# A hybrid decoder layer on one core: the last attention phases' filler work is regrouped around scores and value products

## The chip, the core and the metric

The kernel runs on one core of a Trainium2 chip. A core has a matrix engine (TensorE, PE in the profile, with PEld for its weight loads), a vector engine (DVE), a scalar engine (ACT), GpSimd (POOL) and SyncE (SP), which issues this kernel's transfers. The metric is the device time of one launch in microseconds. It was 1298.78 us as the median of three runs (1298.3 to 1299.28).

## The reference

One decoder layer on 1024 tokens of width 1024, all in float32. A joint projection gives the inputs of two groups of causal attention heads: eight sparse heads (NSA) and four differential heads. Their joined outputs go through an output projection, a residual with layer norm, a SwiGLU feed-forward part of width 2816, and a second layer norm. The change touches the differential heads and what runs beside them:

```python
def diff_attention(q, k, v, lq1, lk1, lq2, lk2, subln_g, slopes, lam_init):
    lam = exp(sum(lq1 * lk1)) - exp(sum(lq2 * lk2)) + lam_init
    ...
    def block(args):                      # one block of 128 query rows
        s = einsum('bqhcd,bkhcd->bhcqk', q_blk, k) * scale
        s = s - slopes[None, :, None, None, None] * dist
        p = masked_softmax(s, dist >= 0)
        a = p[:, :, 0] - lam * p[:, :, 1]
        return einsum('bhqk,bkhe->bqhe', a, v)
    ...
    o = rms_norm(o, subln_g) * (1.0 - lam_init)
...
mix = concatenate([o_diff, o_nsa], axis=-1) @ w_out[l]
x = layer_norm(DEEPNORM_ALPHA * x + mix, ln1_g[l], ln1_b[l])
ffn = (silu(x @ w_gate[l]) * (x @ w_up[l])) @ w_down[l]
x = layer_norm(DEEPNORM_ALPHA * x + ffn, ln2_g[l], ln2_b[l])
```

A head thus has two softmaxes per query block, and their difference is multiplied with the values.

## The kernel before

**Precision.** A product that needs full float32 is split: each operand into a high and a low part, three matmuls per product (`mm3`, lines 116 to 118). `split` writes the parts: a cast on ACT (line 81), a subtraction on DVE or POOL (line 83). `load_split_here` issues the load on SP (line 99) and then splits.

**Units.** The differential attention of head h works in units: one per block i of 128 query rows (row i below), i from 0 to 7, on `(i + 1) * 128` keys. A unit has a front and a back.

- The front makes the scores of both softmaxes into `psS` banks (two matmuls each, lines 331 and 334; past 512 keys in two halves). DVE evacuates each bank with the mask and the row minimum (line 340), ACT takes the exponential (line 354), DVE makes the weight `r1` of the second softmax (lines 475 and 476). The two are then summed: the first five eighths of the width on DVE (line 478), the rest on POOL in two steps (480, 481).
- The back transposes the sum (line 363 into `psT`, ACT copies it, 366), multiplies it with the values into `psO` (line 493), and evacuates the result: DVE copies it (497), ACT sums its squares (498). Behind four rows of a head, `finish` does the RMS norm: small steps on DVE (506 to 508), a power on POOL (509), a multiplication on DVE (510), transposes on TensorE (513), and the store of the transposed rows to `mix_d`.

There are two `psS` banks, two `psM`, three `psT` and one `psO`.

**Fillers.** Other matmuls run beside the units: the projections of q, k and values of later heads, and the output projection of the first rows. Each is a generator that yields after a few matmuls with its cost. `q_fill` (called `qdf` for these heads) projects a q half, ACT scales it (line 176), DVE makes the low part (line 177), and three moves by SP bring the parts to the partitions where the scores read them (line 161). `dvf` projects value rows (matmuls of 256 columns into `psM`). `wo_fill` loads and splits the output weights, `out_fill` makes one block of output rows in two halves of 512 columns, each over `psM`. `held_fill` and `ln_fill` hold back the RMS norms and run layer norms.

**The order.** A table `phases` lists units with their fillers. For each unit the planner calls the front, and runs the back of the unit that is `look` units older; during the back it pumps fillers in proportion to the planned cost of the unit (`ahead`, and `later`, a delay of priority). Units still pending at the end of a phase are carried over to the next. With `passed[0]` a number n, a projection's matmuls are placed behind the score issued n before the last one (`proj_mm3`); with `None` they are free. In the phases marked `even = False`, carried-over units have a weight of zero, so no filler is shared over them. A scheduler then fixes each engine's program from priorities and its own estimate of times; what it makes of the table shows only in the instruction order.

**The last phases** are: head 2 rows 0 to 3; head 3 rows 0 to 3 with the second half of head 2's q and four value rows as fillers; head 2 rows 4, 7, 6, 5 with both halves of w_out, the second half of head 3's q and two blocks of output rows; head 3 rows 4 to 7 with layer norms and two more output blocks. The output projection of the other blocks and the feed-forward part follow.

## Time and profile before

| | before |
|---|---|
| median of three runs | 1298.78 us (1298.3 to 1299.28) |
| the profiled execution, its own time | 1298.14 us |
| its span | 1296.4 us |
| granted TensorE clock, mean | 0.999 |
| PE busy | 1279.8 us, 99% of the span |
| DVE, ACT, POOL busy | 915.7, 651.2, 464.5 us |

The span runs from the first to the last recorded instruction of the profiled execution. In a row of the timeline stand: start in us, duration in us, engine, line of the kernel, operation, output and inputs by the program's names, shape and count, and in brackets the idle time before it with what ended it. In a row of a grouped view stand: line, engine, operation, output and inputs, shape and count, then busy us and the mean ns of one, then the idle time before it. Matmuls are pipelined, and their ends are modelled; so the starts tell more than the durations. "SPq" is SP's queue, where transfers are issued. A matmul of the value product counts twice in the trace's counts (x8 for four).

### The profile page before, as it was taken

To read this page: it belongs to the slowest core of one execution; us is meant where nothing else is said; L and a number is where in the kernel's file an instruction comes from. 1 tells how busy PE (TensorE), PEld (TensorE's weight loads), DVE (VectorE), ACT (ScalarE), POOL (GpSimd) and SP (SyncE) were. 2 spreads that over 40 slices of the span, in tenths; PEclk is the share of its full clock that TensorE was granted. 3 is DMA by queue.
4 is the path that set the end of the run, shared out by engine and by line. 5 is a ranking of instruction groups with operands and counts; after the bars stand their busy time and mean duration, and the time that the engine had idled before them with its cause. 6 is when DMAs were issued, how large, how long until landed. Compare 5 with 4: busy or idle time off the path is not lost.

```text
span 1296.4 us, 20500 instructions
## 1 busy us (share of the span) xinstructions
PE 1279.8 (99%) x6955; PEld 1108.3 (85%) x6955; DVE 915.7 (71%) x1963; ACT 651.2 (50%) x1398; POOL 464.5 (36%) x499
## 2 busy tenths in 40 slices
PE   9999999999999999999999999999999999999997
PEld 7998999998899889788878888888888888888886
DVE  5577886677867556674797777776776768555588
ACT  5377886778766565743344233333333335433330
POOL 4434544454345355643613322322232222000071
PEclk9999999999999999999999999999999999999999
DMA  9411212021122235523224576654554559768641
GB/s 355 134 32 48 48 45 53 26 62 48 34 74 50 70 102 167 175 84 112 82 90 162 178 246 201 202 181 169 167 188 165 195 187 340 265 193 296 193 166 65
DMA packets 86841, 183.13 MB, mean 141 GB/s; under 512 B 10576, under 2 KB 19152, under 8 KB 86608
## 3 DMA queue, kind: packets, MB, share of 16 engines
q1 hardware_dynamic: 86736, 181.82, 43.4%
q8 instruction: 55, 0.90, 0.3%
q14 instruction: 50, 0.41, 0.1%
HBM read 116.18 MB, written 57.15 MB: 134 GB/s over the span
## 4 chain that ended last, share of the span: by engine, by line
PE 94%; DVE 3%; issue 1%; ACT 1%; DMA 0%; POOL 0%; DVEq 0%; ACTq 0%; POOLq 0%
PE psM L116 11%; PE psM L118 11%; PE psM L117 11%; PE psS L118 6%; PE psS L117 6%; PE psS L116 6%; PE psT L116 5%; PE psT L118 5%; PE psT L117 5%; PE psT L373 5%; PE psS L331 4%; PE psS L334 3%; PE psO L436 2%; PE psO L434 2%; PE psO L493 2%; PE psO L118 2%
## 5 line engine op out<-in xcount | busy, mean ns | idle before, releaser
L354 ACT ACTIVATE t<-t,m 128x384 f32<-128x384 f32 (+7 forms) x192 | 144.1, 752 | 59.4 <-DVE m L340 54.7
L419 POOL TENSOR_SCALAR t<-t,r,gates 128x640 f32<-128x640 f32 (+7 forms) x128 | 99.6, 783 | 166.7 <-DVE r L413 116.9
L116 PE MATMUL psM<-big,w 128*128 128x512 f32 x304 | 120.3, 396 | 0.4 <-DVE slot L171 0.3
L118 PE MATMUL psM<-big,w 128*128 128x512 f32 x304 | 119.9, 395 | 0.0
L117 PE MATMUL psM<-big,w 128*128 128x512 f32 x304 | 119.6, 394 | 0.0
L331 PE MATMUL psS<-slot,q 128*128 128x320 f32 (+10 forms) x304 | 110.7, 367 | 3.3 <-DVE m L340 2.5
L1042 POOL TENSOR_TENSOR half<-half,half 128x512 f32<-128x512 f32 x22 | 33.1, 1503 | 203.9 <-ACT half L1041 203.9
L83 DVE TENSOR_TENSOR pt<-psT,pt 128x512 fp32r<-128x512 f32 (+1 forms) x152 | 91.9, 614 | 15.4 <-ACT pt L81 14.7
L334 PE MATMUL psS<-slot,q 128*128 128x320 f32 (+10 forms) x304 | 99.3, 329 | 0.0
L81 ACT CAST pt<-psT 128x512 fp32r<-128x512 f32 (+1 forms) x152 | 77.4, 526 | 24.5 <-PE psT L373 16.5
L81 ACT CAST big<-slot 128x1024 fp32r<-128x1024 f32 (+1 forms) x54 | 54.2, 1018 | 67.5 <-DVE slot L1034 53.6
L83 DVE TENSOR_TENSOR op<-op 128x1024 fp32r<-128x1024 f32 x44 | 61.1, 1395 | 36.5 <-ACT op L81 36.1
L83 DVE TENSOR_TENSOR big<-slot,big 128x1024 fp32r<-128x1024 f32 (+1 forms) x54 | 63.8, 1187 | 29.8 <-ACT big L81 29.6
L373 PE MATMUL psT<-ident,t 128*128 128x128 f32 x528 | 83.7, 273 | 0.1
L81 ACT CAST op<-op 128x1024 fp32r<-128x1024 f32 x44 | 45.9, 1052 | 62.1 <-DMA op<-t_d 59.3
L340 DVE CUSTOM_DVE_ANT_0 t<-psS,dsel 128x384 f32<-128x384 f32 (+9 forms) x128 | 62.5, 493 | 17.3 <-PE psS L334 15.3
L1046 POOL TENSOR_TENSOR half<-half,half 128x512 f32<-128x512 f32 x22 | 36.5, 1658 | 101.5 <-DVE half L1045 101.4
L434 PE MATMUL psO<-pt,slot 128*128 128x256 f32 x264 | 72.2, 288 | 0.0
L436 PE MATMUL psO<-pt,slot 128*128 128x256 f32 x264 | 71.7, 292 | 0.0
L118 PEld LDWEIGHTS psM<-big,w 128*128 128x128 f32 x304 | 57.1, 188 | 11.5
L116 PEld LDWEIGHTS psM<-big,w 128*128 128x128 f32 x304 | 57.3, 188 | 10.7 <-DVE slot L171 0.4
L81 ACT CAST big<-big 128x1024 fp32r<-128x1024 f32 (+1 forms) x49 | 44.2, 912 | 43.4 <-DMA big<-t_d 36.9
(371 smaller groups left out, 3968.9 us busy)
## 6 DMA issues: line engine op xcount, KB each, us to landing
a_d<-slot SPq DMA_DIRECT2D x77, 256.0 KB, 3.0
t_d<-slot SPq DMA_DIRECT2D x77, 256.0 KB, 2.2
q<-q SPq DMA_DIRECT2D x48, 256.0 KB, 2.9
slot<-in_w_up_dram SPq DMA_DIRECT2D x22, 512.0 KB, 3.9
slot<-in_w_down_dram SPq DMA_DIRECT2D x22, 512.0 KB, 3.9
op<-a_d SPq DMA_DIRECT2D x44, 256.0 KB, 3.4
op<-t_d SPq DMA_DIRECT2D x44, 256.0 KB, 4.4
big<-a_d SPq DMA_DIRECT2D x33, 256.0 KB, 3.1
```

The lines of the kernel that those rows point to most:

```text
L81: nc.scalar.copy(hi, src)
L83: eng.tensor_sub(lo, src, hi.bitcast(F32))
L116: nc.tensor.matmul(acc, lhsT=ah, rhs=bh, start=first, stop=False, skip_group_check=more)
L117: nc.tensor.matmul(acc, lhsT=ah, rhs=bl, start=False, stop=False, skip_group_check=more)
L118: nc.tensor.matmul(acc, lhsT=al, rhs=bh, start=False, stop=last, skip_group_check=more)
L331: mm = nc.tensor.matmul(ps[:, :c + part], lhsT=q[0], rhs=k[:, ks], start=True, stop=False)
L334: nc.tensor.matmul(ps[:, :c + part], lhsT=q[1], rhs=k[:, ks], start=False, stop=True)
L354: nc.scalar.activation(t[:, :width], t[:, :width], AF.Exp, bias=m, scale=-1.0, accum_out=r)
L373: nc.tensor.transpose(tp[:rows, n * P:(n + 1) * P], s, ident)
L419: nc.gpsimd.tensor_scalar(t, t, r[:, c:c + 1], gates[:, i, gc:gc + 1], op0=ALU.mult, op1=ALU.mult)
L434: nc.tensor.matmul(po[:, :256], lhsT=v, rhs=pt[:, 0, n * 256:(n + 1) * 256], start=False, stop=False)
L436: nc.tensor.matmul(po[:, :256], lhsT=v, rhs=pt[:, 1, n * 256:(n + 1) * 256], start=False, stop=last)
```

## The change

The table of the last phases is rewritten, with the planner extended for it:

- `passed` is 3 in the phases of head 3 rows 0 to 3 and head 2 rows 4 to 7, where it was `None`: projections stand behind the score issued three before the last one.
- A new column `keep`: in these two phases carried-over units keep their weight, so fillers are shared over them.
- Of head 3's first phase only value row 4 stays as a filler beside head 2's q; value rows 5 to 7 move to the next phase.
- Head 2's rows run 4, 5, 6, 7, with `look` 1 for the first and 2 then, and `ahead` 1.0 for 1.25.
- The output blocks 0 and 1 are issued half by half: the first halves of both, then the second halves.
- `BEHIND`: the scores of head 2's row 5 are placed behind the last value product of head 3's row 3.
- `WHOLE`: for five units (head 3 rows 1 to 3, head 2 rows 4 and 5) DVE sums the whole width, and POOL's two steps are gone. These are the sums of 256, 384, 512, 640 and 768 columns.

All matmuls stay; their order changes from head 2's row 2 on.

```diff
+        BEHIND = {(2, 5): (3, 3)}
+        WHOLE = {(3, 1), (3, 2), (3, 3), (2, 4), (2, 5)}
+        turned = {}
...
                     for c in range(2):
-                        scores(q_of(qt, i, c), kd[c], 0, width, dsel[:, 1024 - width:], slope, m[:, c:c + 1], ts[c])
+                        with ExitStack() as queued:
+                            if (h, i) in BEHIND:
+                                queued.enter_context(tc.issue_after(turned[BEHIND[h, i]]))
+                            scores(q_of(qt, i, c), kd[c], 0, width, dsel[:, 1024 - width:], slope, m[:, c:c + 1], ts[c])
...
-                    cut = width * 5 // 8
+                    cut = width if (h, i) in WHOLE else width * 5 // 8
                     nc.vector.scalar_tensor_tensor(ts[0][:, :cut], ts[1][:, :cut], r1, ts[0][:, :cut],
                                                    op0=ALU.mult, op1=ALU.add)
-                    nc.gpsimd.tensor_scalar(ts[1][:, cut:width], ts[1][:, cut:width], r1, None, op0=ALU.mult)
-                    nc.gpsimd.tensor_add(ts[0][:, cut:width], ts[0][:, cut:width], ts[1][:, cut:width])
+                    if cut < width:
+                        nc.gpsimd.tensor_scalar(ts[1][:, cut:width], ts[1][:, cut:width], r1, None, op0=ALU.mult)
+                        nc.gpsimd.tensor_add(ts[0][:, cut:width], ts[0][:, cut:width], ts[1][:, cut:width])
...
-        def out_fill(i, normed):
+        def out_fill(i, normed, halves=(0, 1)):
             def steps():
-                out_start(i)
-                for nh in range(2):
+                if 0 in halves:
+                    out_start(i)
+                for nh in halves:
                     yield from out_half(i, nh, ps_m())
                 if normed:
                     norm1(i)
-            return steps, 10.4
+            return steps, 5.2 * len(halves)
...
             ([(diff, 3, range(4))],
-             [qdf(2, 1), dvf(1, range(4, 8))], 2, 1.25, 60, None, False),
-            ([(diff, 2, (4, 7, 6, 5))],
-             [wo_fill(0), qdf(3, 1), wo_fill(1), held_fill(), out_fill(0, False), out_fill(1, False)],
-             2, 1.25, 40, None, False),
+             [qdf(2, 1), dvf(1, (4,))], 2, 1.25, 60, 3, False, True),
+            ([(diff, 2, range(4, 8))],
+             [wo_fill(0), dvf(1, (5, 6, 7)), qdf(3, 1), wo_fill(1), held_fill(),
+              *(out_fill(i, False, (nh,)) for nh in range(2) for i in range(2))],
+             (1, 2, 2, 2), 1.0, 40, 3, False, True),
...
-                pending = [(p[0], (0, 0, 0)) for p in pending]
-                beside = [u[2] for u in units][:-1]
+                if not keep:
+                    pending = [(p[0], (0, 0, 0)) for p in pending]
+                beside = [p[1] for p in pending] + [u[2] for u in units][:-1]
```

Three places of the instruction order carry the prediction. The first is TensorE's program at the first score of head 3 (`psS_6629`, from q `q_6618`), and DVE's program where that q is made (line 177). `psS_6527` is the last score of head 2's row 3, `psO_6415` the value product of head 1's row 7; `psM_6716` and, after the change, `psM_6654` are the second half of head 2's q, `psM_6794` is a value row. TensorE before:

```order
L331 MATMUL psS_6527<-slot1_6019,q_6280 128x512
L334 MATMUL psS_6527<-slot1_6019,q_6280 128x512
L493 MATMUL psO_6415<-slot8_3030,pt_6421 128x128 x4
L493 MATMUL psO_6415<-slot9_3389,pt_6432 128x128 x4
L118 MATMUL psM_6794<-slot10_5573,big_158 128x256
L331 MATMUL psS_6629<-slot2_6467,q_6618 128x128
L334 MATMUL psS_6629<-slot2_6467,q_6618 128x128
```

and after the change:

```order
L118 MATMUL psM_6654<-big_163,w_6134 128x512
L331 MATMUL psS_6527<-slot1_6019,q_6280 128x512
L334 MATMUL psS_6527<-slot1_6019,q_6280 128x512
L500 MATMUL psO_6415<-slot8_3030,pt_6421 128x128 x4
L500 MATMUL psO_6415<-slot9_3389,pt_6432 128x128 x4
L331 MATMUL psS_6629<-slot2_6467,q_6618 128x128
L334 MATMUL psS_6629<-slot2_6467,q_6618 128x128
L331 MATMUL psS_6634<-slot4_6468,q_6619 128x128
L334 MATMUL psS_6634<-slot4_6468,q_6619 128x128
L116 MATMUL psM_6654<-big_168,w_6135 128x512
```

Between the last matmul of head 3's q projection and this score, before has the whole second half of head 2's q (24 matmuls of 512 columns) and three matmuls of a value row; after the change only 12 of the 24 stand there, and the other 12 follow the score. DVE before:

```order
L478 SCALAR_TENSOR_TENSOR t_6399<-t_6399,r1_6398 128x160
L177 SCALAR_TENSOR_TENSOR q_6618<-psM_6593,qscale_91,q_6618 128x512
L340 ISA t_6443,m_6441<-psS_6444,dsel_88 128x384
L340 ISA m_6441 128x1
L497 COPY od_6185<-psO_6338 128x128
```

and after:

```order
L484 SCALAR_TENSOR_TENSOR t_6399<-t_6399,r1_6398 128x160
L340 ISA t_6443,m_6441<-psS_6444,dsel_88 128x384
L340 ISA m_6441 128x1
L177 SCALAR_TENSOR_TENSOR q_6618<-psM_6593,qscale_91,q_6618 128x512
L340 ISA t_6443,m_6441<-psS_6449,dsel_88 128x384
```

Line 177 has moved behind the evacuation of a score of 384 columns.

The second place is TensorE's program at the value products of head 3's rows 1 to 3 and the scores of head 2's row 5 (384 columns a half). Before, the products of head 3's rows 2 and 3 and the first four of head 2's row 4 stand among scores:

```order
L493 MATMUL psO_6931<-slot6_5591,pt_6936 128x128 x3
L331 MATMUL psS_7178<-slot0_6018,q_6786 128x384
L334 MATMUL psS_7178<-slot0_6018,q_6786 128x384
L331 MATMUL psS_7183<-slot1_6019,q_6787 128x384
L334 MATMUL psS_7183<-slot1_6019,q_6787 128x384
L117 MATMUL psM_7220<-big_7112,w_7138 128x512
L118 MATMUL psM_7220<-big_7112,w_7137 128x512
L493 MATMUL psO_6973<-slot6_5591,pt_6979 128x128 x4
L331 MATMUL psS_7188<-slot1_6019,q_6787 128x384
L334 MATMUL psS_7188<-slot1_6019,q_6787 128x384
L493 MATMUL psO_7019<-slot6_5591,pt_7025 128x128 x4
```

and after:

```order
L118 MATMUL psM_7135<-big_6876,w_7127 128x512
L363 MATMUL psT_6932<-ident_74,t_6776 128x128 x4
L500 MATMUL psO_6790<-slot6_5591,pt_6794 128x128 x2
L363 MATMUL psT_7048<-ident_74,t_6820 128x128 x4
L500 MATMUL psO_6845<-slot6_5591,pt_6850 128x128 x3
L500 MATMUL psO_6931<-slot6_5591,pt_6937 128x128 x4
L331 MATMUL psS_6993<-slot0_6018,q_6737 128x384
L334 MATMUL psS_6993<-slot0_6018,q_6737 128x384
L331 MATMUL psS_6998<-slot0_6018,q_6737 128x384
L334 MATMUL psS_6998<-slot0_6018,q_6737 128x384
L116 MATMUL psM_6976<-big_163,w_6585 128x512
```

Three value products (`psO_6790`, `6845`, `6931`, the rows 1, 2, 3 of head 3) now stand with four transposes between the first two and nothing between the last two, and the scores of row 5 follow them.

The third place is DVE's program a little later, after the change. `w_7212` is the low part of a half row of the mix for an output block, `psS_7003` the third score bank of row 5, `psS_7020` the first of row 6:

```order
L340 ISA t_6991,m_6989<-psS_6998,dsel_88,m0_6996 128x384
L340 ISA m_6989 128x1
L518 TENSOR_TENSOR od_6729<-od_6729,ss_6730 128x512
L83 TENSOR_TENSOR w_7212<-w_7212,w_7213 128x512
L340 ISA t_6992,m0_7006<-psS_7003,dsel_88 128x384
L340 ISA m0_7006 128x1
L177 SCALAR_TENSOR_TENSOR q_7074<-psM_6976,qscale_91,q_7074 128x512
L340 ISA t_6992,m_6989<-psS_7008,dsel_88,m0_7006 128x384
L340 ISA m_6989 128x1
L340 ISA t_7018,m0_7023<-psS_7020,dsel_88 128x448
```

and before:

```order
L340 ISA m0_6961 128x1
L83 TENSOR_TENSOR w_7259<-w_7259,w_7260 128x512
L340 ISA t_6947,m_6944<-psS_6963,dsel_88,m0_6961 128x512
L340 ISA m_6944 128x1
L177 SCALAR_TENSOR_TENSOR q_7084<-psM_7059,qscale_91,q_7084 128x512
L497 COPY od_6708<-psO_6775 128x128
```

In both, the subtraction of a half row stands ahead of a score's evacuation; it has moved from head 2's row 7 (512 columns a half) to row 5.

More of the change, by code (lines that the diff above doesn't have):

```diff
@@ L492, in back @@
                             c = (j % 4) * 256 + (h % 2) * P
-                            nc.tensor.matmul(po[:, :P], lhsT=pt[:, n * P:(n + 1) * P], rhs=V[j // 4][:, c:c + P],
-                                             start=(j == 0), stop=(j == i))
+                            av = nc.tensor.matmul(po[:, :P], lhsT=pt[:, n * P:(n + 1) * P], rhs=V[j // 4][:, c:c + P],
+                                                  start=(j == 0), stop=(j == i))
                         fill((j4 + len(js)) / (i + 1))
+                    turned[h, i] = av.ins
                     tmp = small([P, P], "ms", 2)
@@ L825, in layer_kernel @@
             ([(nsa, 0, (2, 1, 0, 3, 4, 5, 6, 7))],
-             [vg_fill(3), vg_fill(4), qf(0, 1), vg_fill(5), vg_fill(6), vg_fill(7), qf(1, 0)], 2, 1, 80, 8, True),
+             [vg_fill(3), vg_fill(4), qf(0, 1), vg_fill(5), vg_fill(6), vg_fill(7), qf(1, 0)], 2, 1, 80, 8, True, False),
             ([(nsa, 1, range(8))],
-             [qf(1, 1), kf(0), kf(1), qf(2, 0)], 2, 1, 80, 8, True),
+             [qf(1, 1), kf(0), kf(1), qf(2, 0)], 2, 1, 80, 8, True, False),
             ([(nsa, 2, range(7))],
-             [qf(2, 1), wo_copy(0), dvf(0, range(8)), qf(3, 0)], 2, 1, 60, 8, True),
+             [qf(2, 1), wo_copy(0), dvf(0, range(8)), qf(3, 0)], 2, 1, 60, 8, True, False),
@@ L831, in layer_kernel @@
             ([(nsa, 2, (7,)), (nsa, 3, (1, 0, 2, 3, 5, 4, 6, 7))],
-             [qf(3, 1), wo_copy(1), kdf(0, 0), kdf(0, 1), qdf(0, 0), kdf(1, 0)], 2, 1, 60, 8, True),
+             [qf(3, 1), wo_copy(1), kdf(0, 0), kdf(0, 1), qdf(0, 0), kdf(1, 0)], 2, 1, 60, 8, True, False),
             ([(diff, 0, (2, 1, 0, 3, 5, 4, 6, 7))],
-             [kdf(1, 1), qdf(0, 1), qdf(1, 0), dvf(1, range(4))], 1, 1, 200, 6, True),
+             [kdf(1, 1), qdf(0, 1), qdf(1, 0), dvf(1, range(4))], 1, 1, 200, 6, True, False),
@@ L844, in layer_kernel @@
             ([(diff, 3, range(4, 8))],
[L845 removed]
+             [ln_fill((0, 1)), out_fill(2, True), out_fill(3, True)], 2, 0.9, 60, None, False, False),
         ]
@@ L857, in finish_unit @@
             finish_held()
-        for parts, fillers, look, ahead, later, passed[0], even in phases:
+        for parts, fillers, look, ahead, later, passed[0], even, keep in phases:
             units = [u for make, head, blocks in parts for u in make(head, blocks)]
@@ L892, in pump @@
                     run["due"] += share(work) * rate
-            for front, back, work, needs in units:
+            looks = look if isinstance(look, tuple) else (look,) * len(units)
+            look = looks[-1]
+            for (front, back, work, needs), ahead_of in zip(units, looks):
                 while not needs <= there:
@@ L900, in layer_kernel @@
                 pending.append((back, work))
-                while len(pending) > look:
+                while len(pending) > ahead_of:
                     finish_unit(pump, later)
```

5 lines of the change are left out of this document (2 added, 3 removed).

## The prediction

> **What bounds the kernel now.** I read the page first: span, busy time by engine, the chain that ended last.
>
> ```profile
> span 1296.4 us, 20500 instructions
> PE 1279.8 (99%) x6955; PEld 1108.3 (85%) x6955; DVE 915.7 (71%) x1963; ACT 651.2 (50%) x1398; POOL 464.5 (36%) x499
> PE 94%; DVE 3%; issue 1%; ACT 1%; DMA 0%; POOL 0%; DVEq 0%; ACTq 0%; POOLq 0%
> ```
>
> TensorE is busy for 99% of the span and 94% of the chain. Both kernels hold the same matmuls, so time can come or go only where TensorE waits. The next view is busy time in stretches around the edit; columns are stretch, length, then PE, PEld, DVE, ACT and POOL busy with counts, the granted clock, the DMA share and GB/s.
>
> ```profile
> 800.00:900.00 100.00, 100.00 (x443) 82.84 (x442) 72.77 (x89) 34.47 (x52) 29.54 (x19) 1.00 0.54 178
> 484.00:500.00 16.00, 15.50 (x105) 14.09 (x104) 11.58 (x31) 10.69 (x31) 12.25 (x13) 1.00 0.63 171
> 500.00:526.00 26.00, 26.00 (x175) 23.75 (x174) 13.89 (x50) 15.35 (x46) 10.86 (x14) 1.00 0.63 198
> 526.00:534.00 8.00, 6.82 (x40) 5.35 (x38) 7.20 (x18) 7.55 (x16) 7.81 (x7) 1.00 0.51 137
> 534.00:542.00 8.00, 6.33 (x45) 5.29 (x44) 7.30 (x23) 4.17 (x13) 6.60 (x7) 1.00 0.51 164
> 542.00:560.00 18.00, 18.00 (x114) 16.19 (x113) 13.07 (x38) 10.66 (x28) 5.90 (x7) 1.00 0.28 90
> ```
>
> The first row gives the price of a 512-column matmul in a full stream: 100/443 = 0.226 us from start to start. A busy share of 100% can still hide parts of a wait, because a matmul counts as busy until its modelled end; so I went through the starts. The waits of the phases that change are these.
>
> ```profile
> 494.97 0.36 PE L118 MATMUL psM<-slot,big 128*128 128x256 f32 x1
> 495.84 0.30 PE L331 MATMUL psS<-slot,q 128*128 128x128 f32 x1 [0.50 <-DVE od L497]
> ...
> 527.37 0.37 PE L334 MATMUL psS<-slot,q 128*128 128x448 f32 x1
> 528.84 0.47 PE L331 MATMUL psS<-slot,q 128*128 128x448 f32 x1 [1.10 <-DVE m L340]
> ...
> 535.16 1.11 PE L493 MATMUL psO<-slot,pt 128*128 128x128 f32 x8
> 536.03 0.42 PE L331 MATMUL psS<-slot,q 128*128 128x384 f32 x1
> 536.29 0.34 PE L334 MATMUL psS<-slot,q 128*128 128x384 f32 x1
> 537.11 1.16 PE L493 MATMUL psO<-slot,pt 128*128 128x128 f32 x8 [0.49 <-ACT ms L498]
> ...
> 538.55 0.31 PE L334 MATMUL psS<-slot,q 128*128 128x320 f32 x1
> 539.96 0.63 PE L513 MATMUL psT<-ident,od 128*128 128x128 f32 x4 [1.09 <-DVE r L475]
> ```
>
> Each loss is the distance of two starts less the first one's own streaming time (0.226 scaled by columns): 0.87 - 0.12 = 0.75 before the first score of head 3; 1.47 - 0.20 = 1.27 at 528.84; 0.82 - 0.17 = 0.65 at 537.11; 1.41 - 0.15 = 1.26 at 539.96. Smaller ones between them, found in the same way, add 1.2 to 1.6. So before loses 0.75 at 495.8 and 1.27 + 0.65 + 1.26 + 1.4 = **4.6 us between 526 and 542**, and next to nothing from 500 to 526 and from 542 to 560.
>
> **The first term: the move of head 3's q.** L177 writes that q, three moves by SP spread it over both partition halves, and the first score of head 3 waits for the last move.
>
> ```profile
> 485.44 1.01 DVE L476 SCALAR_TENSOR_TENSOR r<-r,lam,r 128x1 f32<-128x1 f32 x1
> 486.49 1.38 DVE L478 SCALAR_TENSOR_TENSOR t<-t,r 128x160 f32<-128x160 f32 x1
> 487.79 0.74 DVE L177 SCALAR_TENSOR_TENSOR q<-psM,qscale,q 128x512 fp32r<-128x512 f32 x1
> 488.45 0.55 DVE L340 CUSTOM_DVE_ANT_0 t<-psS,dsel 128x384 f32<-128x384 f32 x1
> ...
> 488.56 4.68 SPq L161 DMA_DIRECT2D q<-q  x3
> ```
>
> L177 ends at 488.53, the score starts at 495.84: 7.3 us for the moves, two abreast and a third issued when they have landed. The row's label names the DVE copy, but that was long done. In before 24 matmuls of 512 columns and three of 256 stand between the projection's last matmul and this score, beside scores, transposes and value products. After the change the same scores and products stand there with 12 of the 512 columns alone. So TensorE arrives 12 x 0.226 + 3 x 0.113 = 3.05 us sooner at a wait that ends no sooner. On DVE, L177 now stands behind one more 384-column score (0.55 us in the row above), which ends the wait later by up to that. Bounds 3.0 (L177 not delayed) to 3.6 (all of it); I take **+3.3**, so a wait of about 4.1 us in all. Part of it may show at a score ahead of this one, whose bank waits for DVE; the sum is the same.
>
> **The second term: the old waits go.** The scores of head 2's rows 6 and 5 and of head 3's row 4 (448, 384 and 320 columns a half), packed between 526 and 542, are now spread, with up to 15 projection matmuls between them. The waits there lie between neighbours that the change parts: **-4.6**, at least -3.2 should the fragments (1.4) come back.
>
> **The third term: new neighbours.** The products of head 3's rows 1, 2 and 3 (2, 3 and 4 matmuls) now stand one behind the other, with four transposes ahead of the second and nothing ahead of the third, because the scores of head 2's row 5 are bound behind row 3's last product. There is one psO bank: each row's product waits until DVE has copied and ACT squared the one before.
>
> ```profile
> 536.31 0.29 DVE L497 COPY od<-psO 128x128 f32<-128x128 f32 x1
> ...
> 536.69 0.28 ACT L498 ACTIVATE ms<-psO 128x128 f32<-128x128 f32 x1 [0.44 <-DVE od L497]
> ```
>
> Before shows that chain at 537.11: copy from 536.31, square from 536.69, next product 0.80 after the copy's start, and the copy itself starts some 0.4 after the last product's start, about 1.2 us in all. Ahead of the third product only the last matmul's own 0.1 to 0.2 covers it: 1.0 lost. Ahead of the second, four transposes at about 0.11 cover more: 0.6 lost at the least, 1.5 if DVE's whole-width sum (640 columns, below) or a cast on ACT stands ahead of the copy; I take 1.0. Together **+2.0** (1.5 to 2.5).
>
> Next, the pair that made the wait at 528.84 comes back: a subtraction of a half row of the mix (L83) stands on DVE ahead of a score's L340.
>
> ```profile
> 526.40 1.71 DVE L83 TENSOR_TENSOR w<-w 128x512 fp32r<-128x512 f32 x1 [1.17 <-ACT w L81]
> 528.04 0.74 DVE L340 CUSTOM_DVE_ANT_0 t<-psS,dsel,m 128x512 f32<-128x512 f32 x1
> 521.06 1.25 ACT L81 CAST big<-big 128x512 fp32r<-128x512 f32 x2 [1.05 <-DMA big<-wo_d]
> ```
>
> L83 waits for ACT's cast, which stands behind casts of w_out that wait for their loads. After the change such an L83 stands ahead of the L340 of the third score of row 5, whose bank row 6's first score takes. Price between 0 (cast early) and the 1.27 of before, or somewhat more: I take **+1.2**. Three smaller places (a projection bank waiting for L177; ACT's casts ahead of exponentials; transposes close behind the whole-width sum of row 5) have 0 to 0.9 each; I take 0.4 to 0.5 for each, **+1.4**.
>
> The five sums made whole on DVE: 640 columns took 1.03 us where they were five eighths, POOL's share of 384 took two steps.
>
> ```profile
> 533.42 1.03 DVE L478 SCALAR_TENSOR_TENSOR t<-t,r 128x640 f32<-128x640 f32 x1
> L480 POOL TENSOR_SCALAR t<-t,r 128x384 f32<-128x384 f32 x2 | 3.2, 1590 | 0.4 <-DVE r L476 0.4
> L481 POOL TENSOR_TENSOR t<-t 128x384 f32<-128x384 f32 x2 | 2.0, 1016 | 0.1
> ```
>
> Whole, row 5 of head 2 (768 columns) takes about 1.03 x 768/640 = 1.24 us of DVE instead of some 0.8 beside 2.0 on POOL: sooner for the transposes, 0.4 later for DVE's next scores. It comes to nothing in the sum, because DVE has 5 to 12 us free in the stretches at 500 and 542; without that cover, the 960 columns moved cost 960 x 1.03/640 = 1.5 us.
>
> One row above is out of line: L476, on one column, took 1.01 us, while its median is 0.22.
>
> ```profile
> L476 DVE SCALAR_TENSOR_TENSOR r<-r,lam,r x32: 206/219/1014, 388.9 to 575.6; 128x1 f32<-128x1 f32 x32
> 483.89 3.79 POOL L83 TENSOR_TENSOR big<-big 128x512 fp32r<-128x512 f32 x3
> ```
>
> POOL was in a run of subtractions at that moment. [...]
>
> **The last term: the tail.** The output rows of head 3's last four rows are transposed 12 matmuls (2.7 us) after the last product instead of some 40. Before, they came 9 us behind it:
>
> ```profile
> 590.99 1.95 PE L493 MATMUL psO<-slot,pt 128*128 128x128 f32 x16
> ...
> 601.68 0.60 PE L513 MATMUL psT<-ident,od 128*128 128x128 f32 x4
> ```
>
> The chain between them (copy, square, two DVE steps, the power on POOL, the multiplication) is the one that ended at 539.96, where it ran 3.65 us from the copy at 536.31, some 4.0 from the last product's start. Less 2.7 and that product's own 0.1 to 0.2: 1.1 to 1.2. Bounds 0 (POOL and DVE free at once) and 2.5 (POOL in a long row of a layer norm); I take **+1.0**.
>
> **Sum.** 3.3 - 4.6 + 2.0 + 1.2 + 1.4 + 1.0 = +4.3 us. The profiled execution took 1298.14 us (1.74 around its span), so 1302.4; the median of the runs, 1298.78, lies 0.64 above it. I predict **1302.4**. What a measurement of this kernel can tell from no change is 0.2%, 2.6 us, so the sum lies above that bound by 1.7.
>
> **Rivals.** *No change* (0.25): the move's wait is there, but the third term stops at the psO bank, which is all that the order forces: 3.3 - 4.6 + 2.0 = +0.7, 1298.8, up to +2.6 with the tail and one more wait. For it: TensorE's waits from 500 to 526 were nil with the same kind of neighbours; against it: L83 and the casts have the same order that cost 1.27.
>
> *Faster* (0.09): L177 comes sooner. It ended at 488.53 because L476 and L478 were slow while POOL ran, the first by 0.8 us, the second by 1.0: of two such, with a mean of 0.88, the other took 0.38.
>
> ```profile
> L478 DVE SCALAR_TENSOR_TENSOR t<-t,r 128x160 f32<-128x160 f32 x2 | 1.8, 880 | 0.1
> ```
>
>  If POOL's subtractions fall elsewhere, the moves end 1.8 us sooner, the first term is 3.3 - 1.8 = 1.5, and with the bank's 1.0 as the only other wait the sum is 1.5 - 4.6 + 1.0 = -2.1 to -3.1 with none on the bank, 1295.0 to 1296.0. It decides where the move's wait falls under 2.3 us in all. Against it: SP's third move and the casts keep their order, and POOL has the same subtractions before it.
>
> *Clock* (0.06, within slower). The longest wait above is 1.27 us and the granted clock stays 1.00 there; behind the last matmul it falls:
>
> ```profile
> 1288.99 0.28 PE L118 MATMUL psS<-op 128*128 128x256 f32 x1
> ...
> 1293.00:1296.40 3.40, 0.00 (x0) 0.00 (x0) 0.29 (x1) 0.00 (x0) 0.00 (x0) 0.57 0.42 154
> ```
>
> The stretch from 1293.0, 4 us behind it, has a mean of 0.57, so an idle of about 4 us is enough. If the 4.1 us come in one piece and the clock halves for some 3 us behind it, that is 1.5 to 3 more: 1304 to 1305.5. [...] I hold it less likely, since scores ahead of the move take part of the wait.
>
> *That the sums or binds don't happen* I rule out: the order of both kernels shows them.
>
> **Chances.** Forecast 0.66 (the clock's 0.06 with it), no change 0.25, faster 0.09; these are also slower, within 0.2%, faster. The forecast's own range, from its bounds (3.0 to 3.6; -4.6 to -3.2; 1.5 to 2.5; 0 to 1.3; 0 to 2.7; 0 to 2.5, seldom all at one end), is 1300.5 to 1305.4; down into the no-change case the range for 8 in 10 is 1298.7 to 1305.4.
>
> **What would show it.** Right: some 4 us without starts of matmuls between 486 and 497 in the changed profile, ending at head 3's first score; no waits among the scores of rows 5 to 7 of head 2; two waits of about 1 us ahead of products of head 3's rows 2 and 3; some 8 us fewer of POOL (five of each of its two steps), 1.5 more of DVE. Wrong: if the score of head 3 starts without a wait of over 2 us, or if the third term's waits are absent, the time is at or below before's.

## The result

The changed kernel took 1311.48 us, the median of four runs (1310.11 to 1314.90), beside 1298.93 for the kernel before (1298.30 to 1299.28): a ratio of 1.0101, 95% interval 1.0081 to 1.0121. It is slower by 12.6 us, where I forecast 3.6 more than the median, in a range that ended at 1305.4. The direction was right, the size was not.

The page of the changed kernel, the lines that answer to those of before:

```profile
span 1310.2 us, 20487 instructions
PE 1284.1 (98%) x6955; PEld 1109.9 (85%) x6955; DVE 913.2 (70%) x1963; ACT 652.2 (50%) x1398; POOL 457.1 (35%) x489
```

The same number of matmuls, 13.8 us more of span; POOL is 7.4 us less busy. Busy time by stretch, of the changed kernel, with the columns of the prediction:

```profile
484.00:500.00 16.00, 12.06 (x73) 10.37 (x72) 9.54 (x30) 9.99 (x32) 12.29 (x13) 1.00 0.53 153
526.00:534.00 8.00, 5.55 (x28) 4.89 (x27) 2.14 (x8) 3.06 (x11) 3.31 (x3) 0.79 0.22 73
534.00:542.00 8.00, 7.14 (x38) 5.78 (x37) 4.26 (x9) 5.38 (x12) 4.67 (x5) 1.00 0.74 239
542.00:560.00 18.00, 15.77 (x80) 12.38 (x80) 12.30 (x30) 10.15 (x22) 6.63 (x6) 1.00 0.53 157
605.00:630.00 25.00, 23.71 (x128) 19.64 (x127) 9.57 (x15) 7.91 (x15) 8.14 (x8) 1.00 0.34 116
664.00:690.00 26.00, 23.54 (x129) 19.12 (x128) 25.04 (x40) 14.38 (x26) 5.27 (x4) 1.00 0.25 90
```

POOL's 7.4 us fewer were forecast (some 8); the 1.5 us more of DVE were not seen, its sum is 2.5 us lower. Two things are new. The granted clock is 0.79 in the row from 526. And time is lost in rows behind the attention, at 605 and at 664. In the changed kernel the line numbers are a little higher than in the one before (the value product is L500, its square on ACT L506, the sum L484, the transposes of the RMS norm L521). In TensorE's timeline the waits stand singly; the number ahead of the arrow is the idle time that the view counts, somewhat less than the loss from start to start that I use.

```profile
489.41 0.50 PE L331 MATMUL psS<-slot,q 128*128 128x512 f32 x1 [1.69 <-DVE m L340]
497.38 0.30 PE L331 MATMUL psS<-slot,q 128*128 128x128 f32 x1 [2.25 <-DMA q<-q]
528.29 0.94 PE L500 MATMUL psO<-slot,pt 128*128 128x128 f32 x6 [1.67 <-ACT ms L506]
530.01 1.81 PE L500 MATMUL psO<-slot,pt 128*128 128x128 f32 x8 [0.79 <-ACT ms L506]
539.91 0.47 PE L331 MATMUL psS<-slot,q 128*128 128x448 f32 x1 [0.86 <-DVE m L340]
545.02 0.47 PE L331 MATMUL psS<-slot,q 128*128 128x448 f32 x1 [0.40 <-DVE m L340]
546.48 0.85 PE L363 MATMUL psT<-ident,t 128*128 128x128 f32 x6 [0.79 <-DVE t L484]
548.08 0.50 PE L116 MATMUL psM<-big,w 128*128 128x512 f32 x1 [0.29 <-ACT w L81]
549.58 0.50 PE L116 MATMUL psM<-big,w 128*128 128x512 f32 x1 [0.76 <-ACT w L81]
617.02 0.50 PE L116 MATMUL psM<-big,w 128*128 128x512 f32 x1 [0.48 <-ACT w L81]
619.03 0.63 PE L521 MATMUL psT<-ident,od 128*128 128x128 f32 x4 [0.81 <-DVE od L518]
669.98 0.63 PE L949 MATMUL psT<-ident,half 128*128 128x128 f32 x4 [1.35 <-DVE half L968]
```

Loss by place, both kernels, from the distance of starts less a matmul's streaming time (0.226 us at 512 columns, scaled by columns), in us:

| place | before | changed | my term | measured difference |
|---|---|---|---|---|
| move of head 3's q (489.41, 497.38) | 0.75 | 1.85 + 2.42 | +3.3 | +3.5 |
| the waits of before between 526 and 542 | 4.5 | gone | -4.6 | -4.5 |
| single psO bank (528.29, 530.01) | - | 1.83 + 0.95 | +2.0 | +2.8 |
| clock at half speed for 3.4 us | - | 1.7 | 0 | +1.7 |
| bank of row 6's first score (539.91) | - | 1.0 | +1.2 | +1.0 |
| smaller places (545.02 to 549.58) | - | 0.6 + 0.95 + 0.45 + 0.9 | +1.4 | +2.9 |
| tail (617.02, 619.03) | - | 0.65 + 1.0 | +1.0 | +1.6 |
| start of the feed-forward part, 664 to 700 | 1.9 | 4.0 | 0 | +2.1 |
| first 10 us, same program in both | - | 1.0 | 0 | +1.0 |

These make 12.1 of the 13.8 us; the rest are waits below 0.3 us. The last row belongs to this one execution: the same first instructions ran with a late load, before anything that was changed. In the other profiles the same stretch is longer than in the one of before by anything from 0 to 1.7 us.

### The profile page after: what moved, and what is told of

It is laid out like the page before. It is cut to its first block, busy times and chain, and to the rows that moved or that the text cites. A ratio compares the mean times of both kernels' runs of the same rounds, so it can differ in the third digit from the quotient of the medians.

```text
span 1310.2 us, 20487 instructions
## 1 busy us (share of the span) xinstructions
PE 1284.1 (98%) x6955; PEld 1109.9 (85%) x6955; DVE 913.2 (70%) x1963; ACT 652.2 (50%) x1398; POOL 457.1 (35%) x489
## 4 chain that ended last, share of the span: by engine, by line
PE 89%; DVE 4%; DMA 3%; issue 2%; POOL 1%; ACT 1%; SPq 0%; DVEq 0%; POOLq 0%; ACTq 0%
PE psM L116 10%; PE psM L117 10%; PE psM L118 10%; PE psT L116 5%; PE psT L118 5%; PE psT L117 5%; PE psS L118 5%; PE psS L117 5%; PE psS L116 5%; PE psT L373 5%; PE psS L331 4%; PE psS L334 3%; PE psO L436 2%; PE psO L434 2%; PE psO L500 2%
## 5 line engine op out<-in xcount | busy, mean ns | idle before, releaser
L83 DVE TENSOR_TENSOR pt<-psT,pt 128x512 fp32r<-128x512 f32 (+1 forms) x152 | 91.8, 614 | 15.4 <-ACT pt L81 14.8
L83 DVE TENSOR_TENSOR op<-op 128x1024 fp32r<-128x1024 f32 x44 | 61.2, 1400 | 37.2 <-ACT op L81 36.7
L83 DVE TENSOR_TENSOR big<-slot,big 128x1024 fp32r<-128x1024 f32 (+1 forms) x54 | 63.9, 1189 | 28.6 <-ACT big L81 28.4
L331 PEld LDWEIGHTS psS<-slot,q 128*128 128x128 f32 x304 | 57.7, 190 | 12.8 <-DVE m L340 6.7
L118 PEld LDWEIGHTS psM<-big,w 128*128 128x128 f32 x304 | 57.3, 188 | 11.1
```

Of the source, the lines that this page charges most:

```text
L83: eng.tensor_sub(lo, src, hi.bitcast(F32))
L118: nc.tensor.matmul(acc, lhsT=al, rhs=bh, start=False, stop=last, skip_group_check=more)
L331: mm = nc.tensor.matmul(ps[:, :c + part], lhsT=q[0], rhs=k[:, ks], start=True, stop=False)
```

## The experiments

All runs stand beside runs of the kernel before on the same chip (medians 1299.09 to 1299.39, and 1298.93 beside the changed kernel). A difference to the changed kernel's 1311.48 is therefore uncertain by some 0.5 us besides the spread of the runs, which is wide for the changed kernel (1310 to 1315); the section on the hardware comes back to that.

### The first phase's binding alone

```diff
-[qdf(2, 1), dvf(1, (4,))], 2, 1.25, 60, 3, False, True
+[qdf(2, 1), dvf(1, (4,))], 2, 1.25, 60, None, False, True
```

> One edit undone: in the phase of head 3's rows 0 to 3 the projections are free again (None where the change has 3); all else as changed. The order then has 11.1 us of matmuls between head 3's q projection and its first score, as before the change, where the change has 8.0; the products of head 3's rows 1 to 3, the tail and the order behind it stay as in the changed kernel. Theory (the binding of this phase makes the move's wait, 4.3 us in the changed kernel in two pieces against 0.75 before): the two waits fall to about 1 us and the time by 3 to 3.6, to about 1308 from 1311.5. Rival (the wait is made by DVE's later L177, or by value rows 5 to 7 moved out of the phase): the waits stay above 2.5 us and the time moves by less than 1.

Measured: 1309.89 us (1308.08 to 1310.15), 1.0079 of before (1.0064 to 1.0094). TensorE's timeline of this run:

```profile
491.98 0.40 PE L331 MATMUL psS<-slot,q 128*128 128x512 f32 x1
496.48 0.30 PE L331 MATMUL psS<-slot,q 128*128 128x128 f32 x1 [0.56 <-DMA q<-q]
```

The two waits of 4.3 us are one of 0.8 (496.48). So the binding of that phase makes the wait, by 11.1 against 8.0 us of matmuls ahead of the score, as the prediction had it. The time fell by 1.6 only, less than the theory's 3 to 3.6. From the last wait ahead of the edit to the cast's wait in the tail this profile takes 137.5 us (475.70 to 613.22), that of the changed kernel 140.9 (476.13 to 617.02): 3.4 less, of which 1.7 (3.41/2, as an estimate) is the clock, which stayed at 1.00 in this execution from 523.14 to 529.97, around its waits at the psO bank. What the move gave, new waits between 500 and 546 took back in half.

### The scores of row 5 not behind row 3

```diff
-BEHIND = {(2, 5): (3, 3)}
+BEHIND = {}
```

> One edit undone: the scores of head 2's row 5 are not placed behind head 3's row 3 (BEHIND empty). The order then has 0.85 us and more of matmuls between the products of head 3's rows 1 to 3. Theory (the bare neighbourhood of three products on one psO bank costs 1.8 + 0.95 us of waits, and these two, close together, halve the clock for 3.4 us, 1.7 us more): the waits there fall under 1 us in all, the clock stays 1.00, the time falls by 3 to 4.5, to about 1307.5. Rival (the first of the two waits is ACT's cast standing idle for its w_out load, whatever stands between the products): a wait of over 1 us stays ahead of a product or a score in this stretch, and the time falls by 1 or less.

Measured: 1305.07 us (1304.86 to 1306.61), 1.0048 (1.0032 to 1.0065): 6.4 less, more than the theory's 4.5. No product waits between 526 and 542 any more. But the theory's clock doesn't hold: amid new waits of 0.93 us (a score at 542.68) and 1.36 (the RMS norm's transposes at 544.45) half speed sets in: the granted clock is 0.50 from 544.20 to 547.61. And w_out's loads, which stand behind the last use of the input's tiles, are issued earlier than in the changed kernel. SP's queue in the changed kernel, in this run, and before:

```profile
520.89 0.80 SPq L99 DMA_DIRECT2D big<-wo_d  x2
...
534.17 4.38 SPq L99 DMA_DIRECT2D big<-wo_d  x6
```

```profile
521.75 2.18 SPq L99 DMA_DIRECT2D big<-wo_d  x4
...
526.21 2.20 SPq L99 DMA_DIRECT2D big<-wo_d  x4
```

```profile
516.06 3.53 SPq L99 DMA_DIRECT2D big<-wo_d  x6
...
523.68 0.93 SPq L99 DMA_DIRECT2D big<-wo_d  x2
```

The last six go out at 534.2 to 538.6 in the changed kernel, all eight by 528.4 and 524.6 in the others. So the binding did two things: it piled up the products, and it pushed back the last projection that reads the tiles w_out is to land in. The rival, that a wait of over 1 us stays whatever stands between the products, can't be judged from this run, since the loads came earlier too.

### Whole output blocks

```diff
-*(out_fill(i, False, (nh,)) for nh in range(2) for i in range(2))],
+out_fill(0, False), out_fill(1, False)],
```

> One edit undone: the two output blocks are made one after the other again, not half by half. The order then has 7.7 us of matmuls between the last value product and the last head's transposes (2.7 in the changed kernel, 8.8 before), and DVE's order in the output stage and at the start of the feed-forward part is again that of before. Theory (the 4.2 us lost from 605 to 720 come from that order): the waits there fall from 7.6 to about 3.3 us, the time by 4, to about 1307.5. Rival (they come from the whole run being later by 8 us against its loads): the waits stay, the time moves by less than 1.

Measured: 1312.44 us (1307.21 to 1313.17), 1.0093 (1.0072 to 1.0114). The waits from 605 to 720 fell from 7.6 to 4.6 us, not to 3.3, and the time didn't fall. In the profiled execution TensorE lost, as an estimate, up to 5.1 us (three times 3.41/2) to three windows at a granted clock of 0.50 (below), two more than in the changed kernel's, and one wait grew to 2.5 us. Its quickest run, 1307.21, is what the theory expected; the median isn't. Taken alone, this run settles nothing; the half blocks on the kernel before, further down, do.

### The waits at the psO bank filled with matmuls

```diff
+                        if (h, i) in ((3, 2), (3, 3)):
+                            with tc.issue_after(turned[h, i - 1]):
+                                for _ in range(1):
+                                    busy = ps_s()
+                                    for _ in range(7 if i == 2 else 4):
+                                        nc.tensor.matmul(busy[:, :P], lhsT=ident, rhs=ident, start=True, stop=True)
```

> The changed kernel with matmuls that nobody reads put into the two waits at the single psO bank: 7 behind the product of head 3's row 1 and 4 behind that of row 2, 1.6 and 0.9 us of TensorE, no more than the 1.8 and 0.95 us it waits there. All else stays in its order. Theory (two waits within 3.4 us halve the granted clock for the next 3.4 us, which costs 1.7): the clock stays 1.00 through this stretch, and the time falls by about 1.5, to 1310, though work was added. Rival (the lower clock there is an accident of one execution): the time stays or rises by up to 0.3, and runs spread as widely as the changed kernel's (1310 to 1315).

Measured: 1310.13 us (1309.22 to 1311.29), 1.0084 (1.0069 to 1.0099): 1.35 less, with some 2.4 us of matmuls more, though the runs of both kernels overlap. Here the stretch stays at full speed, but half speed comes 10 us later, behind a score's wait that had grown to 2.0 us:

```profile
526.80:530.00 3.20, 3.20 (x28) 2.92 (x27) 0.29 (x1) 2.11 (x7) 2.50 (x2) 1.00 0.08 22
...
536.77:540.18 3.41, 1.56 (x6) 0.78 (x6) 3.09 (x6) 3.41 (x9) 3.07 (x3) 1.00 0.58 198
540.18:543.59 3.41, 3.41 (x9) 2.62 (x9) 2.67 (x5) 2.35 (x5) 3.10 (x3) 0.50 0.83 198
```

Work put into a wait cost nothing here. That it is what held the clock in that place is not shown by this profile alone: the run without the first phase's binding kept full speed there as well, with both waits unfilled. Nor are the times of the two told apart.

### The first phase as before

```diff
-[qdf(2, 1), dvf(1, (4,))], 2, 1.25, 60, 3, False, True
+[qdf(2, 1), dvf(1, (4, 5, 6, 7))], 2, 1.25, 60, None, False, False
...
-[wo_fill(0), dvf(1, (5, 6, 7)), qdf(3, 1), ...
+[wo_fill(0), qdf(3, 1), ...
```

> The phase of head 3's rows 0 to 3 as before the change: value rows 5 to 7 are back in it, its projections free, no share over carried-over units; the rest as changed. Theory (besides the move's wait, the value rows that moved into the next phase keep the input's tiles in use, into whose place w_out is loaded; so ACT's casts of w_out stand idle for their loads ahead of the squares, and the casts of the mix rows come late): the first wait at the psO bank falls from 1.8 us to at most 1.0, the waits at 539.9 and from 545 to 550 (3.9 us in all) to under 2, and with the 3.3 of the move's wait the time falls by 5 to 7, to 1305 or 1306. Rival (only the move's wait hangs on this phase): the time falls by 1.5 to 3.5, as when its binding alone was undone (1309.9), and the casts still wait by 1 us and more for w_out.

Measured: 1303.26 us (1302.33 to 1304.62), 1.0030 (1.0020 to 1.0040): 8.2 less, the most that one part gave. SP's queue and TensorE's products here:

```profile
517.89 5.12 SPq L99 DMA_DIRECT2D big<-wo_d  x8
```

```profile
530.97 0.94 PE L500 MATMUL psO<-slot,pt 128*128 128x128 f32 x6 [0.41 <-ACT ms L506]
532.69 1.16 PE L500 MATMUL psO<-slot,pt 128*128 128x128 f32 x8 [0.78 <-ACT ms L506]
```

All eight loads are issued by 523.0, and the first wait at the bank is 0.57 us instead of 1.83, though the products stand as close as before; the second keeps its 0.95. That is the bound that I gave the first (0.6) and the value of the second. What had made the first longer is on ACT in the changed kernel:

```profile
527.35 0.62 ACT L81 CAST big<-big 128x512 fp32r<-128x512 f32 x1 [0.99 <-DMA big<-wo_d]
527.88 0.27 ACT L506 ACTIVATE ms<-psO 128x128 f32<-128x128 f32 x1
```

The copy of that product had ended at 526.5, and the square came at 527.88, behind a cast that stood idle for its load. The waits behind it shrink too, as the theory had it: the one of 539.9 is gone, and of the four from 545 to 550 (2.9 us) there remain 0.45 and 0.57, at 542.2 and 543.9; and full speed is kept: the first two matmuls of the score behind the products start 0.26 and 0.18 us ahead of the next (533.60, 533.86), where at half speed the changed kernel has 0.46 and 0.32 (531.47, 531.93). The rival is out: more than the move hangs on this phase. The run changes the value rows, the binding and the sharing of that phase at once; which of them makes the loads late is for the last experiment.

### The sums divided again, and the sums whole alone

```diff
-WHOLE = {(3, 1), (3, 2), (3, 3), (2, 4), (2, 5)}
+WHOLE = set()
```

> One edit undone: the five sums are divided again, five eighths on DVE, the rest on POOL. TensorE's order at the products of head 3's rows 1 to 3 stays, the last transposes stand 1.8 us behind the last product (2.7 in the changed kernel). Theory (the whole-width sums cost nothing, since DVE has nothing else to do there): waits at the move, the psO bank and the casts as in the changed kernel, the tail 0.9 longer, the time within 1.5 of 1311.5. Rival (the sum of row 5, 1.45 us ahead of its transposes, and those of 640 columns ahead of the copies make the waits): the time falls by 2 or more.

Measured: 1313.07 us (1311.22 to 1313.57), 1.0101 (1.0086 to 1.0116), with the tail's wait at 1.55 instead of 1.0 us: just over the theory's upper end (1313.0), and not lower, as the rival had it. And on the kernel before, the same five sums made whole (`cut = width` for them, POOL's steps left out):

> The kernel before with one part of the change: the five sums whole on DVE. The order of TensorE stays but for details (the tail has 8.1 us of matmuls where it had 8.8). Theory (the sums cost nothing): 1299, within 1 us of the kernel before. [...]

Measured: 1299.44 us beside 1299.39, 0.9999 (0.9990 to 1.0009). No cost or gain of the whole sums shows. The interval reaches from 1.3 us less to 1.2 more, so a gain or a cost below that is not seen, but not ruled out either.

### Three parts undone at once

The first phase as before, `BEHIND` empty, whole output blocks, with the edits above.

> The changed kernel with three parts undone at once: the phase of head 3's rows 0 to 3 as before, no binding behind row 3, whole output blocks. What is left of the change: rows 4 to 7 of head 2 in order, look 1 then 2, the binding to scores and the sharing in that one phase, the whole-width sums. Theory (the losses sit in the three parts: 3.5 at the move and more through the late loads, 4.5 at the bank with the clock, 4.2 in the tail and behind it): the time falls to 1297 to 1300, beside the kernel before. Rival (what is left is at fault as well): 1302 or more, with waits of over 2 us in all among the scores of rows 5 to 7.

Measured: 1299.91 us (1299.32 to 1302.45), 1.0005 (0.9996 to 1.0015): the kernel before again. What is left of the change (row order, look, the one bound and shared phase, the whole sums) shows no loss by itself, and the loss sits in the three parts. They aren't additive: undone singly they gave 8.2, 6.4 and nothing, together 11.6. Two of them hold up the same loads, as SP's queue showed, which fits this.

### A wait put into a full stream

On the kernel before, in the last product of the feed-forward part, with 5 and with 12 copies into a tile that nobody reads:

```diff
+                if j == 2 and p == 5:
+                    junk = const.tile([P, P], F32, name="junk")
+                    d = ps_o()
+                    with tc.issue_after(last):
+                        nc.tensor.matmul(d[:, :P], lhsT=ident, rhs=ident, start=True, stop=True)
+                    for _ in range(5):        # 12 in the second kernel
+                        nc.scalar.copy(junk, d[:, :P])
+                    last = nc.tensor.matmul(d[:, :P], lhsT=ident, rhs=ident, start=True, stop=True).ins
+                with ExitStack() as queued:
+                    if j > 2 or j == 2 and p >= 5:
+                        queued.enter_context(tc.issue_after(last))
...
```

> The kernel before with one wait put into a full stream of TensorE, in the last product of the feed-forward part: a small matmul, five copies of its result by ACT, and a second small matmul that may overwrite it only then; all that follows stands behind the second. The copies take about 0.2 us each, with 0.5 us around them: a wait of about 1.5 us. [...]

Measured: 1301.71 us (1301.14 to 1302.20, eleven runs), 1.0017 (1.0008 to 1.0026). The wait was 1.7 us against the 1.5 expected, the two small matmuls, which I had left out, took some 0.4, and 2.3 are lost, with the eleven runs in a single heap. No window ran at half speed among the work of the profiled execution: from 1276.20 to 1279.64 TensorE was busy for 2.62 us, from 1279.64 to 1283.05 for 2.69, both at 1.00.

> The same with twelve copies: a wait of about 3 us. [...] Rival (the price of a wait is its length): all runs at 3 us more, with the spread of the kernel before (1 us).

Measured: 1306.05 us (1304.26 to 1306.96, five runs), 1.0049 (1.0035 to 1.0063). The wait was 3.8 us, longer than planned: seven copies more brought the second small matmul's start from 1.93 to 4.02 us behind the first one's, so 0.3 us a copy where 0.2 was expected. Two runs, with a mean clock of 0.998, took 1304.26 and 1305.02; three, at 0.996, took 1306.05 to 1306.96. So the same wait costs 4.9 to 5.6 us, or 6.7 to 7.6. The profiled one is of the second kind:

```profile
1277.24:1280.65 3.41, 1.37 (x8) 0.98 (x6) 3.27 (x6) 1.81 (x7) 0.32 (x1) 1.00 0.39 147
1280.65:1284.07 3.42, 1.82 (x5) 1.59 (x6) 2.93 (x6) 1.39 (x6) 0.92 (x1) 0.50 0.12 38
1284.07:1287.48 3.41, 3.41 (x9) 2.64 (x8) 0.00 (x0) 0.00 (x0) 0.00 (x0) 0.50 0.35 127
```

The window in which the wait ended (at 1282.25) and the one behind it ran at half speed, so the price is more than the wait's length, and the rival falls. The means of the two kinds are 2 us apart; but five runs, with gaps of 0.8 us inside the groups and 1.0 between them, don't show two groups as such; the mean clock alone divides them.

### The half blocks alone

On the kernel before, `out_fill` and the list of fillers as in the change.

> The kernel before with one part of the change: the two output blocks are made half by half. The order then has value products 0.6 and 1.0 us of matmuls apart in two places (0.35 in one before), 7.2 us of matmuls ahead of the last transposes (8.8 before), and DVE's order in the output stage is another. Theory (that order brings waits of its own at the start of the feed-forward part, 4.0 us in the changed kernel from 664 to 700 against 1.9): slower by 1 to 3, 1300 to 1302, with the waits from 660 to 700 at 3 us or more. Rival (they come with the tail's delay alone): within 1 of the kernel before.

Measured: 1302.36 us (1301.78 to 1303.29), 1.0022 (1.0012 to 1.0032): 3.0 slower, where whole blocks in the changed kernel showed no gain. But only half is where the theory put it: the waits from 630 to 720 are 4.5 us (3.1 before), 1.4 more; those from 542 to 560 are 2.4 against 0.4, in small pieces among the scores. And the changed kernel's longest wait there, 1.5 us at 669.98 for a subtraction on DVE, isn't among them: the half blocks alone don't make it.

### Late value rows without the bindings

The first phase's binding, `BEHIND` and the half blocks undone, value rows 5 to 7 left in the later phase.

> The changed kernel with the first phase's binding, the binding behind row 3 and the half blocks undone, but value rows 5 to 7 left in the later phase (and the sharing in both). It differs from the kernel with three parts undone (1299.9) by those value rows and the sharing in the first phase. Theory (the value rows keep the input's tiles, so w_out lands late and ACT's casts hold up what stands behind them): waits of 2 us or more in all from 535 to 550 with casts idle for w_out or mix rows, the time 1301.5 to 1304. Rival (the value rows' place costs nothing once the bindings are gone): 1299 to 1300.5.

Measured: 1302.69 us (1301.14 to 1304.88), 1.0028 (1.0017 to 1.0039). The time is in the theory's range, which is luck, for its cause isn't there: between 526 and 550 no cast waits for w_out. The longest wait is one for the RMS norm:

```profile
543.59 0.63 PE L521 MATMUL psT<-ident,od 128*128 128x128 f32 x4 [1.97 <-DVE od L518]
...
539.09 1.83 POOL L487 TENSOR_SCALAR t<-t,r 128x384 f32<-128x384 f32 x1 [0.31 <-DVE ss L516]
540.89 1.03 POOL L517 TENSOR_TENSOR ss<-ss,mhalf 128x4 f32<-128x4 f32 x1
```

POOL's power (L517) stands behind a step of a divided sum of head 2's row 7. So the value rows alone don't bring w_out late: its last loads go out by 526.0, by 524.7 in the run with three parts undone. It takes the binding behind row 3 as well, for with both, and the first phase's binding undone, the last six go out from 530.0 to 533.6. The binding alone doesn't do it either: with it, and the first phase as before, all were out by 523.0.

## Why the prediction was wrong

**The first term** (+3.3, measured +3.5) was right, place and mechanism: fewer matmuls ahead of a wait whose end is fixed by three moves. The run without the binding showed it.

**The second term** (-4.6) was right: those waits are gone.

**The third term** was mis-sized: 2.0 + 1.2 + 1.4 predicted, 2.8 + 1.0 + 2.9 measured. The step that failed is how I treated the bounds. I had the first wait at the bank between 0.6 and 1.5, "1.5 if ... a cast on ACT stands ahead of the copy", and the smaller ones at 0 to 0.9 each, and took the middle of each, as if they were independent. Most of them hang on one thing, w_out's loads being late: the first wait came out over its upper end (1.83; the cast stood ahead of the square, not of the copy), and the smaller places at 2.9 in all, in four pieces (0.56, 0.95, 0.45 and 0.93), over the upper ends of the three I had counted. With the loads early these shrank to 0.57 and 1.0, while the second wait at the bank kept the 0.95 that I had given it. The last two of the four pieces wait for casts of mix rows, whose loads (from 544.35) stand late in SP's queue behind the same delay; that this delay is w_out's alone is argued, not shown. I had read in the order that ACT's casts stand ahead, and not asked when their data lands: the last six loads went out from 534.2 to 538.6, where the last of before went out by 524.6.

Adding the upper ends would not have been enough: they sum to +9.4 (3.6 - 3.2 + 2.5 + 1.3 + 2.7 + 2.5), which is 1307.5. Of the 7.8 us by which the table's 12.1 exceed the sum's 4.3, 2.1 lie in the third term; 1.7 (the clock) and 2.1 (the start of the feed-forward part) lie in two terms that the sum put at nothing, 0.6 in the tail, 0.3 in the first two terms, and 1.0 in the first 10 us, which belong to the execution.

**The clock** was not in the sum. I held it as a rival, 0.06, with a wrong condition in a wrong place: an idle of 4 us in one piece, at the move. The move's 4.3 us left the clock at 1.00 in the profiled execution; two waits of 1.83 and 0.95 us with some 0.7 of work between them were followed by half speed for 3.41 us, which cost 1.7 (half of it, as an estimate):

```profile
526.92:530.33 3.41, 1.26 (x8) 1.07 (x9) 0.29 (x1) 2.25 (x7) 2.28 (x2) 1.00 0.22 68
530.33:533.74 3.41, 3.41 (x14) 3.23 (x13) 1.47 (x5) 0.37 (x2) 0.77 (x2) 0.50 0.00 0
```

So "time can come or go only where TensorE waits" was not the whole of it: the 3.4 us behind these waits are a full stream, and cost, by this estimate, 1.7 us more than at full speed.

**The tail** (+1.0, measured +1.6) was of the right kind: the wait for the RMS norm was 1.0, and a wait for a cast ahead of it added 0.65.

**What was missing**: the start of the feed-forward part, +2.1. The sum has no term for it; the source there is the same in both kernels, but the order isn't. In the changed kernel two steps of a layer norm (L663) stand ahead of the subtraction (L968) that feeds the transposes at 669.98; in the kernel before, the subtraction comes first. Changed, then before:

```profile
667.83 1.40 DVE L663 SCALAR_TENSOR_TENSOR slot<-slot,mv,slot 128x512 f32<-128x512 f32 x2
669.15 0.68 DVE L968 TENSOR_TENSOR half<-slot,slot 128x512 f32<-128x512 f32 x1
```

```profile
651.10 0.68 DVE L955 TENSOR_TENSOR half<-slot,slot 128x512 f32<-128x512 f32 x1
...
653.46 1.40 DVE L654 SCALAR_TENSOR_TENSOR slot<-slot,mv,slot 128x512 f32<-128x512 f32 x2
```

The order of both kernels shows it; I read it only as far as the last transposes of the attention. It is not the half blocks alone that turn the two round. The wait of 1.5 us stands in the profiles that have both the half blocks and the binding behind row 3 (the changed kernel, the runs with the first phase's binding undone, the waits filled, the first phase as before and the sums divided). It is in none that has only one of them (the half blocks alone, `BEHIND` empty, whole blocks). Why the two together do it stays open.

**The rivals**: *no change* needed a third term that stops at the bank; it didn't. Of the signs named, "no waits among the scores of rows 5 to 7" failed: 1.0 and 0.56 us stand there, the first of them in the third term's own place. The sums took 2.1 us more of DVE (23.8 against 21.7) where 1.5 was worked out, though DVE's total fell. *Faster* needed an earlier L177. In the kernel before, the six L476 that ran beside POOL's subtractions (L83) took 0.34 to 1.01 us, the other 26 took 0.21 to 0.26 (in the changed kernel one beside L83 took 0.22, at 544.15). In the changed kernel the two instructions ahead of L177 ran beside L83 again and were as slow as before (0.98 and 1.35 us), and L177 ended at 490.0 instead of 488.5: 0.95 of that from the first 10 us, 0.55 from the score ahead of it, as the first term's upper bound had it.

```profile
486.52 0.98 DVE L482 SCALAR_TENSOR_TENSOR r<-r,lam,r 128x1 f32<-128x1 f32 x1
487.53 1.35 DVE L484 SCALAR_TENSOR_TENSOR t<-t,r 128x160 f32<-128x160 f32 x1
488.81 0.54 DVE L340 CUSTOM_DVE_ANT_0 t<-psS,dsel 128x384 f32<-128x384 f32 x1
...
489.28 0.74 DVE L177 SCALAR_TENSOR_TENSOR q<-psM,qscale,q 128x512 fp32r<-128x512 f32 x1
```

## What to carry to other kernels

Where an engine in order serves both a load and a chain that the bound engine waits for, ask for each such instruction when its data lands, and not only where it stands; waits that share one late load can reach their upper ends together, and the range has to allow for it. Where a scheduler orders the program, a local edit can move instructions 100 us behind it: compare the order to the end. And a wait of TensorE can be dearer than its length: the 3.8 us put in cost 4.9 to 7.6 us here, with half speed behind it.

## What the runs showed of the hardware

In the trace of the kernel before, the record of the granted clock begins at 6.65 us with 1.00 and falls to 0.50 at 1293.48; in that of the changed kernel it begins at 8.09, falls at 530.33, rises at 533.74 and falls at 1305.15. The distances are 377, and 153, 1 and 226 times 3.4133 us; such a stretch is called a window here. The half-speed stretch among the work is one window long in the changed kernel, and two in the run with the long wait (1280.65 to 1287.48). In the run with whole blocks half speed began at 496.93, 531.06 and 554.96: 10 and 7 windows apart. In the windows ahead of it TensorE was busy (the first number behind the length) for 1.24, 1.12 and 1.08 us:

```profile
493.52:496.93 3.41, 1.24 (x12) 1.05 (x10) 1.52 (x6) 1.18 (x4) 1.72 (x4) 1.00 0.55 118
496.93:500.34 3.41, 3.29 (x10) 2.84 (x11) 1.96 (x11) 0.99 (x4) 1.62 (x3) 0.50 0.71 272
527.65:531.06 3.41, 1.12 (x8) 0.74 (x6) 0.37 (x2) 2.05 (x7) 1.72 (x2) 1.00 0.39 128
531.06:534.48 3.42, 3.17 (x13) 3.18 (x14) 0.71 (x2) 0.56 (x4) 0.81 (x1) 0.50 0.00 0
```

Of the windows at full speed that I read, the busiest that half speed followed had 1.69 us (the run with `BEHIND` empty), the least busy that it didn't follow 1.73 (the changed kernel), 0.50 and 0.51 of 3.41. The edges are placed to some 0.03 us, and a matmul's end is modelled, so the two can't be told apart:

```profile
540.79:544.20 3.41, 1.69 (x10) 1.04 (x8) 3.13 (x6) 2.16 (x4) 2.97 (x3) 1.00 0.82 265
...
485.99:489.40 3.41, 1.73 (x14) 1.43 (x12) 3.01 (x6) 1.89 (x6) 3.41 (x5) 1.00 0.49 154
```

The long wait put in has one window with 1.82 followed by half speed, but that one ran at half speed itself, where the same matmul is busy for longer (there 0.43 us from start to start, at 1283.3, against 0.227). Half speed for a window costs, as an estimate from its length and the clock of 0.50, 3.41/2 = 1.7 us of a full stream. Where the windows fall against the program differs between these executions: the first edge is at 6.65 us in the trace of the kernel before and at 8.09 in the changed kernel's, and the q move left a window with 1.24 us busy in the run with whole blocks (above) and 1.15 in the one with the sums divided, but two with 2.3 and 2.2 in the changed kernel's, with the same waits. The waits at the psO bank, 1.76 and 0.95 us in the run without the first phase's binding, fell into two windows there, and full speed stayed:

```profile
523.14:526.55 3.41, 1.82 (x15) 1.50 (x14) 0.29 (x1) 2.35 (x6) 1.07 (x1) 1.00 0.50 169
```

That the changed kernel's runs spread over 5 us where those of the kernel before beside them spread over 1 fits this, as does the mean clock of 0.996 in its slowest and 0.998 in its quickest; it wasn't tried by itself beyond the two waits put in.
